# A hybrid mixer layer on one core: the sums of the second half's x^T are formed in the first half and kept in DRAM

## The chip, the cores and the metric

The kernel runs on one NeuronCore of one Trainium2 chip. The metric is the device time of one execution in microseconds (us), as the median of several runs. TensorE (PE) multiplies matrices, VectorE (DVE), ScalarE (ACT) and GpSimd (POOL) work on tiles, and SyncE (SP) issues nearly all DMA transfers, one queue in program order.

## The reference, cut to what matters

```
xn = rms_norm(x, ln_g)                        # x: (2048, 1024)
proj = xn @ w_in                              # w_in: (1024, 6144), six groups of 1024 columns
b_gate, c_gate, x_conv, g_conv, x_lru, g_lru = split(proj)
y_conv = norm(b_gate * conv3(c_gate * x_conv)) * silu(g_conv)
y_lru  = norm(rg_lru(x_lru)) * silu(g_lru)    # a scan over the 2048 positions
h = x + concat(y_conv, y_lru) @ w_out         # w_out: (2048, 1024)
return rms_norm(h, final_g)
```

## The kernel before, in words

The large products are done in float32 by a scheme of Strassen's kind: a product of 2x2 blocks needs seven products of sums of blocks instead of eight. One operand is the *set* T, the other the weights S. A set holds, for j = 0 to 3, seven *parts* (i, j), each 128x512, made from the four blocks b11, b12, b21, b22 of a pair of row blocks (row blocks j and j+4 of x^T, two halves of 512 positions):

- parts 0, 4 and 5 are b11, b21 and b22 themselves;
- part 3 is b22-b12, part 2 is b12-b11, part 1 is b22 minus part 2, part 6 is b21 minus part 1.

Each part is *split* into two float32r tiles: ACT casts it to `th` (a CAST, "hi"), DVE subtracts to get the rest `tl` (a TENSOR_TENSOR at L160, "lo"). Three matmuls (s.th, s.tl, s.th) per part and j make the product; all are at L877, 128x512 each.

The work is a list of 64 steps: 24 for the first half of the positions (for k = 0 to 7 a step "l" for the linear recurrent unit, "a" and "b" for the short convolution), 24 for the second half, 16 of the output projection. Each half, and each half of the output projection, has its own set T; where one follows the other the set *changes*. A step has seven or eight slots, each starting with `tick()`, which runs the functions that `at(slots, f)` put down some slots earlier. All engines run in the order in which this code issues their instructions. In a steady step the slots multiply parts 0, 6 (of the step before), 1, 3, 2, 4, 5 in turn. ACT copies the intermediate products out of PSUM to q1, u2 and rr. These are single buffers: the copy to u2 of the next step must wait until DVE has read the old u2 (in `put(21, ...)`, the operation `gb<-bank,u` for a step "b"), and PE must wait for that copy before it goes on adding to the same bank.

**x^T of the second half.** In the first half, `second_half` reads the rows of the second half of x (`rows`), gets their norms (`root`, stored to DRAM as `rsx`), and then in 16 calls of `cols(c, kt)`, four in every 21 slots (one k), loads a broadcast of the norms and one block of x^T, scales it on DVE (L515) and stores it to `xnd`. So `xnd` holds the 16 scaled blocks.

**The change to the second half's set.** During the two steps ahead of it and in its first step, `load_t` loads the four blocks of a j from `xnd`, and `TPrep` forms the sums on DVE and splits the parts. j = 0 is spread over the slots of the last step of the first half; j = 1 to 3 are done by `whole()` inside the first step of the new half. That first step (`if jm:`) goes through j from 0 to 3 in the outer loop, with six PSUM banks open, so that PE can start with the parts of j = 0.

**The changes to the two sets of the output projection** use `TParts` instead: there the sums of the weight blocks lie ready in DRAM, each part is loaded into one of eight `raw` buffers (name `traw`), and `parts(n)` splits the parts up to the n-th, two at a time (two casts, two subtractions), and loads up to six parts ahead. Their order puts twelve parts, of j = 0 and 1, ahead of the first step.

The tag `hl` has four 128x1024 buffers, which `st`, `qh`, `ql` of the steady steps share with `xcol`; `aux` has four 128x512 buffers. The last slots of a step "b" and the first of the next "l" carry, on DVE and behind each other: the gates and the scan of the recurrent unit, the splits of the next weights, and the reads of PSUM.

Of the kernel before, what the change touches and what calls it, by code (L numbers as in the profile page):

```python
# [12 lines left out]
F32 = mybir.dt.float32  # L13
# [25 lines left out]
def hymba_kernel(ctx: ExitStack, tc: tile.TileContext, x, xt, w_in, par, lamc, w_gate, w_out, final_g, out):  # L39
# [16 lines left out]
    xnd = [dram.tile([KT, P, C], F32, name=f"xnd{c}") for c in range(2)]  # L56
# [173 lines left out]
    class TPrep:  # L230
# [3 lines left out]
        def add(self, i):  # L234
            b11, b12, b21, b22 = (self.r.get(n) for n in range(4))
            t = self.t
            if i == 2:
                t[2] = aux("t1")
                tt(t[2], b12, b11, ALU.subtract)
            elif i == 1:  # L240
                t[1] = aux("t2")
                tt(t[1], b22, t[2], ALU.subtract)
            elif i == 3:
                tt(b12, b22, b12, ALU.subtract)
            else:
                tt(t[1], b21, t[1], ALU.subtract)


        def whole(self):
            b11, b12, b21, b22 = (self.r[n] for n in range(4))  # L250
            self.t = {1: b22, 2: b11, 6: b21}
            for i in (0, 5, 4):
                self.hi(i)
            self.lo(0)
            tt(b11, b12, b11, ALU.subtract)
            self.lo(5)
            tt(b12, b22, b12, ALU.subtract)
            self.hi(2)
            self.hi(3)
            tt(b22, b22, b11, ALU.subtract)  # L260
            self.hi(1)
            self.lo(4)
            self.lo(1)
            tt(b21, b21, b22, ALU.subtract)
            self.hi(6, b21)
            self.lo(3)
            self.lo(2)
            self.lo(6, None, b21)

# [189 lines left out]


    def load_t(j, r, only=range(4)):
        for n in only:
            i, q = ((0, 0), (0, 1), (1, 1), (1, 0))[n]
            kt = j + i * NB
            r[2 * i + q] = piece("traw")
            nc.sync.dma_start(r[2 * i + q], xnd[q][kt])
# [28 lines left out]
    def second_half():  # L495
# [13 lines left out]
        def cols(c, kt):  # L509
            t2 = wt("hl", "xcol", bufs=HL)  # L510
            rb, t = t2[:, 0:C], t2[:, C:2 * C]
            nc.sync.dma_start(rb.rearrange("p (b q) -> p b q", b=NB),
                              rsx[c].rearrange("(o b) p -> o b p", o=1).broadcast_to((P, NB, P)))
            nc.sync.dma_start(t, xt[kt * P:(kt + 1) * P, (2 + c) * C:(3 + c) * C])
            at(3, lambda: nc.vector.scalar_tensor_tensor(  # L515
                out=t, in0=t, scalar=pt[:, LN_G + kt:LN_G + kt + 1], in1=rb,
                op0=ALU.mult, op1=ALU.mult))
            at(5, lambda: nc.sync.dma_start(xnd[c][kt], t))
# [392 lines left out]
    with tc.manual_schedule(engines={ENG.PE, ENG.Activation, ENG.DVE, ENG.Pool, ENG.SP}):  # L911
# [173 lines left out]
        for n in range(PLAIN, N):  # L1085
# [9 lines left out]
            if jm:  # L1095
                bk = {}
                for j in range(NB):
# [6 lines left out]
                    if Tq is not None and j < 3:  # L1104
                        Tq.parts((14, 21, 28)[j])
                    elif j == 0:
                        Tp[0].hi(6)
                        Tp[0].lo(6)
                        load_t(2, Tp[2].r)
                    elif j == 1:  # L1110
                        load_t(3, Tp[3].r)
                    if Tq is None and j < 3:
                        Tp[j + 1].whole()
# [25 lines left out]
            for s in range(8 if new or last else 7):  # L1139
# [15 lines left out]
                if nx == 1:  # L1155
                    if soon and s == 4:
                        Tp = [TPrep(q, {}, T2) for q in range(NB)]
                        load_t(0, Tp[0].r)
                    if new:
                        if s == 1:  # L1160
                            Tp[0].hi(0)
                            Tp[0].lo(0)
                        elif s == 2:
                            for q in (2, 1, 3):
                                Tp[0].add(q)
                        elif s == 3:
                            load_t(1, Tp[1].r)
                            Tp[0].hi(1)
                        elif s == 4:
                            Tp[0].hi(3)  # L1170
                            Tp[0].lo(1)
                        elif s == 5:
                            Tp[0].hi(2)
                            Tp[0].lo(3)
                            Tp[0].add(6)
# [96 lines left out]
```

## Time and profile before

| | before |
|---|---|
| median of 3 runs | 1426.95 us (1425.71 to 1427.22) |
| the profiled execution | 1426.31 us, span 1424.5 us |
| PE busy | 1335.4 us, 94% of the span |
| DVE busy | 1069.8 us, 75% |
| ACT, POOL busy | 782.0 us (55%), 258.4 us (18%) |
| DMA | 371.02 MB, mean 260 GB/s |
| mean granted TensorE clock | 0.982 |

Busy shares are means over stages with different limits; a stage is read from the windows and from the instructions in order of time. "Idle before, released by" in square brackets names what an engine waited for. In the window lines the columns are the window, its length, the busy time and count of PE, weight loads, DVE, ACT and POOL, then the granted TensorE clock (1.00 is full), the busy share of the DMA engines and GB/s.

### The profile page before, as it was taken

To read this page: it belongs to the slowest core of one execution; us is meant where nothing else is said; L and a number is where in the kernel's file an instruction comes from. 1 tells how busy PE (TensorE), PEld (TensorE's weight loads), DVE (VectorE), ACT (ScalarE), POOL (GpSimd) and SP (SyncE) were. 2 spreads that over 40 slices of the span, in tenths; PEclk is the share of its full clock that TensorE was granted. 3 is DMA by queue.
4 is the path that set the end of the run, shared out by engine and by line. 5 is a ranking of instruction groups with operands and counts; after the bars stand their busy time and mean duration, and the time that the engine had idled before them with its cause. 6 is when DMAs were issued, how large, how long until landed. Compare 5 with 4: busy or idle time off the path is not lost.

```text
span 1424.5 us, 16977 instructions
## 1 busy us (share of the span) xinstructions
PE 1335.4 (94%) x5732; PEld 1068.4 (75%) x5732; DVE 1069.8 (75%) x1264; ACT 782.0 (55%) x1165; POOL 258.4 (18%) x168
## 2 busy tenths in 40 slices
PE   5979999999999997899998999899996999989997
PEld 4867777778787775677886878687874788868885
DVE  5788887998989889777767667665657548668885
ACT  6576668566665756475563645463646323434442
POOL 2414343434534331001000000101010000000000
PEclk9999999999999998999999999999998999989999
DMA  5137797987978866631899999998978999698643
GB/s 212 30 110 259 271 275 239 284 322 273 328 275 297 305 246 220 225 102 38 276 313 339 332 342 326 347 315 307 288 269 330 348 292 278 215 403 292 216 156 122
DMA packets 165190, 371.02 MB, mean 260 GB/s; under 512 B 17264, under 2 KB 52464, under 8 KB 165104
## 3 DMA queue, kind: packets, MB, share of 16 engines
q1 hardware_dynamic: 164672, 369.63, 75.7%
q8 instruction: 45, 0.74, 0.2%
q14 instruction: 41, 0.34, 0.1%
q10 hardware_dynamic: 432, 0.32, 0.1%
HBM read 224.45 MB, written 145.43 MB: 260 GB/s over the span
## 4 chain that ended last, share of the span: by engine, by line
PE 63%; DVE 11%; DMA 10%; ACT 10%; issue 3%; SPq 2%; POOL 0%; DVEq 0%; ACTq 0%
PE bank L877 59%; DVE s L160 2%; ACT i L668 2%; PE gate L661 2%; DMA traw<-in_w_out_dram 2%; ACT r L668 2%; PE norm_ps L554 2%; DVE tl L160 2%; DMA sd<-s 1%; DVE traw L160 1%; DVE r L695 1%; DMA zr<-rsd 1%; DMA so<-so 1%; DMA s<-sd 1%; ACT q L1208 1%
## 5 line engine op out<-in xcount | busy, mean ns | idle before, releaser
L877 PE MATMUL bank<-th,s 128*128 128x512 f32 x3608 | 1145.6, 394 | 43.1 <-DMA s<-so 8.8
L877 PEld LDWEIGHTS bank<-th,s 128*128 128x128 f32 x3608 | 683.4, 189 | 207.5 <-issue 14.5
L877 PE MATMUL bank<-tl,s 128*128 128x512 f32 x1804 | 709.7, 393 | 7.1 <-DVE tl L160 6.5
L877 PEld LDWEIGHTS bank<-tl,s 128*128 128x128 f32 x1804 | 341.7, 189 | 83.2 <-DVE tl L160 11.7
L160 POOL TENSOR_TENSOR s<-raw,s 128x512 fp32r<-128x512 f32 x67 | 127.2, 1911 | 263.2 <-ACT s L197 217.1
L197 ACT CAST s<-raw 128x512 fp32r<-128x512 f32 x136 | 81.9, 617 | 56.9 <-PE bank L877 39.8
L1211 ACT COPY u<-bank 128x512 f32<-128x512 f32 x58 | 34.0, 587 | 140.1 <-PE bank L877 90.2
L160 POOL TENSOR_TENSOR gb<-gb,sg 128x1024 f32<-128x1024 f32 x16 | 42.5, 2658 | 352.4 <-ACT sg L594 296.1
L160 DVE TENSOR_TENSOR s<-s,s 128x512 fp32r<-128x512 f32 x102 | 100.6, 986 | 5.4 <-ACT s L197 5.4
L160 DVE TENSOR_TENSOR tl<-traw,th 128x512 fp32r<-128x512 f32 x98 | 66.5, 705 | 46.9 <-ACT th L454 29.4
L160 DVE TENSOR_TENSOR s<-raw,s 128x512 fp32r<-128x512 f32 (+1 forms) x115 | 86.6, 777 | 9.9 <-ACT s L197 5.3
L1208 ACT COPY q<-bank 128x512 f32<-128x512 f32 x58 | 33.8, 583 | 83.0 <-PE bank L877 75.8
L160 DVE TENSOR_TENSOR raw<-raw,zr 128x512 f32<-128x512 f32 x64 | 47.9, 769 | 36.8 <-DMA zr<-rsd 36.8
L197 ACT CAST s<-s 128x512 fp32r<-128x512 f32 x102 | 62.8, 616 | 7.5 <-DVE s L160 7.4
L635 DVE SCALAR_TENSOR_TENSOR u<-xl,pt,u 128x1024 f32<-128x1024 f32 x48 | 65.4, 1363 | 0.7 <-ACT u L631 0.2
L1214 ACT COPY rr<-bank 128x512 f32<-128x512 f32 x58 | 33.9, 584 | 45.7 <-PE bank L877 45.6
L745 DVE SCALAR_TENSOR_TENSOR t<-p,pt,t 128x1024 f32<-128x1024 f32 x32 | 48.5, 1517 | 4.9 <-ACT t L742 4.1
L160 DVE TENSOR_TENSOR st<-u,st 64x1024 fp32r<-64x1024 f32 x32 | 50.9, 1590 | 1.0
L160 POOL TENSOR_TENSOR gl<-gl,sg 128x1024 f32<-128x1024 f32 x16 | 45.6, 2849 | 14.4 <-ACT sg L594 14.4
L631 ACT ACTIVATE u<-xl,pt 128x1024 f32<-128x1024 f32 x16 | 19.9, 1246 | 48.1 <-DVE xl L160 48.0
L160 DVE TENSOR_TENSOR ob<-bank,rr 128x512 f32<-128x512 f32 x18 | 12.2, 689 | 44.7 <-ACT rr L1214 44.7
L668 ACT ACTIVATE r<-gate,pt 64x512 f32<-64x512 f32 x64 | 43.7, 683 | 1.7 <-PE gate L661 1.1
(161 smaller groups left out, 1372.2 us busy)
## 6 DMA issues: line engine op xcount, KB each, us to landing
sd<-s SPq DMA_DIRECT2D x147, 512.0 KB, 4.8
s<-sd SPq DMA_DIRECT2D x147, 512.0 KB, 6.0
raw<-in_w_in_dram SPq DMA_DIRECT2D x108, 256.0 KB, 4.7
so<-so SPq DMA_DIRECT2D x42, 512.0 KB, 6.2
s<-so SPq DMA_DIRECT2D x42, 512.0 KB, 7.5
raw<-yd SPq DMA_DIRECT2D x64, 256.0 KB, 5.8
traw<-in_w_out_dram SPq DMA_DIRECT2D x56, 256.0 KB, 5.9
yd<-gl SPq DMA_DIRECT2D x32, 256.0 KB, 3.7
```

What stands on the lines that cost most here:

```text
L160: (eng or nc.vector).tensor_tensor(out=out, in0=a, in1=b, op=op)
L197: nc.scalar.copy(dst[i][0], val(i))
L554: nc.tensor.matmul(norm_ps[0], sel[:, s0:s0 + R], q[:, i * C:(i + 1) * C], start=norm_ps[1] == 0, stop=norm_ps[1] == 8 * KT - 1)
L631: nc.scalar.activation(out=v["u"], in_=o1[:, 1:1 + N2], func=AF.Identity, scale=lw[0], bias=pt[:, LB + k:LB + k + 1])
L635: nc.vector.scalar_tensor_tensor(out=v["u"], in0=o1[:, 1 + j:1 + j + N2], scalar=lw[j], in1=v["u"], op0=ALU.mult, op1=ALU.add)
L661: nc.tensor.matmul(ps[j], v["gw"][n][:, j, :], v["st"][j][:, sl], start=(n == 0), stop=(n == 1))
L668: nc.scalar.activation(out=g_[hi, sl], in_=v["ps"][j][src], func=AF.Sigmoid, bias=pt[src, bias + k:bias + k + 1])
L745: nc.vector.scalar_tensor_tensor(out=tcur["t"], in0=p[:, 2 + j:2 + j + N2], scalar=cw[j], in1=tcur["t"], op0=ALU.mult, op1=ALU.add)
L877: nc.tensor.matmul(bank, a[:, js], b, start=start and n == 0, stop=stop and n == 2, skip_group_check=more)
L1208: nc.scalar.copy(q1, bk["A"])
L1211: nc.scalar.copy(u2, bk["A"])
L1214: nc.scalar.copy(rr, bk["A"])
```

## The change

`cols` is replaced by `block(j)`, called four times, once in the step "b" of each k from 3 to 6 (slot 3). It loads both halves of x^T's row blocks j and j+4 and of the norms' broadcast into three `xcol` buffers (six DMAs of 256 KB), scales two 128x1024 tiles on DVE two slots later (`scale`), forms the four sums with four 128x512 subtractions one slot after that (`add`), and stores the seven parts in four DMAs two slots later (`store`). `xnd[j]` now holds seven parts. The change to the second half's set uses `TParts`, which loads each part ready to split; with n = 1 its order puts the seven parts of j = 0 first, then j = 1, 2, 3. `TPrep.add`, `TPrep.whole` and `load_t` are gone.

```diff
-    xnd = [dram.tile([KT, P, C], F32, name=f"xnd{c}") for c in range(2)]
+    xnd = [dram.tile([7, P, C], F32, name=f"xnd{j}") for j in range(NB)]
...
     class TParts:
-            self.order = [(i, j) for i in ORDER for j in range(2)]
-            self.order += [(i, j) for j in (2, 3) for i in ORDER]
+            n = 1 if t == 1 else 2
+            self.order = [(i, j) for i in ORDER for j in range(n)]
+            self.order += [(i, j) for j in range(n, NB) for i in ORDER]
...
-                w = w_blocks(self.t, j)
-                src = {0: w[0], 4: w[2], 5: w[3]}.get(i)
+                w = w_blocks(self.t, j) if self.t > 1 else None
+                src = {0: w[0], 4: w[2], 5: w[3]}.get(i) if w else xnd[j][(0, 3, 4, 5, 2, 1, 6).index(i)]
...
-        def cols(c, kt):
-            ...
+        def block(j):
+            a, b, r = [wt("hl", "xcol", bufs=HL) for _ in range(3)]
+            for c in range(2):
+                cs = slice(c * C, (c + 1) * C)
+                nc.sync.dma_start(r[:, cs].rearrange("p (b q) -> p b q", b=NB),
+                                  rsx[c].rearrange("(o b) p -> o b p", o=1).broadcast_to((P, NB, P)))
+                for t, kt in ((a, j), (b, j + NB)):
+                    nc.sync.dma_start(t[:, cs], xt[kt * P:(kt + 1) * P, (2 + c) * C:(3 + c) * C])
+            def scale():
+                for t, kt in ((a, j), (b, j + NB)):
+                    nc.vector.scalar_tensor_tensor(out=t, in0=t, scalar=pt[:, LN_G + kt:LN_G + kt + 1],
+                                                   in1=r, op0=ALU.mult, op1=ALU.mult)
+            def add():
+                ...
+                tt(t2, b12, b11, ALU.subtract)
+                tt(b12, b22, b12, ALU.subtract)
+                tt(t1, b22, t2, ALU.subtract)
+                x_.append(aux("t6"))
+                tt(x_[0], b21, t1, ALU.subtract)
+            def store():
+                for n, t in enumerate((a, b, r)):
+                    nc.sync.dma_start(xnd[j][2 * n:2 * n + 2].rearrange("h p c -> p h c"),
+                                      t.rearrange("p (h c) -> p h c", h=2))
+                nc.sync.dma_start(xnd[j][6], x_[0])
+            at(2, scale)
+            at(3, add)
+            at(5, store)
...
-        for c in range(2):
-            for kt in range(KT):
-                at(free.pop(1) - 7, lambda c=c, kt=kt: cols(c, kt))
+        for j in range(NB):
+            at(21 * (3 + j) + 17 - 4, lambda j=j: block(j))
...
-                    if Tq is not None and j < 3:
+                    if j < 3:
                         Tq.parts((14, 21, 28)[j])
-                    ...
-                    if Tq is None and j < 3:
-                        Tp[j + 1].whole()
...
-                if nx == 1:
-                    ...
+                if nx:
                     if soon and s == 5:
                         Tq = TParts(nx, T2)
                         Tq.load(4)
                     if new and s in (1, 3, 4, 5, 6, 7):
-                        Tq.parts(2 * (1, 3, 4, 5, 6, 7).index(s) + 2)
+                        Tq.parts(((1, 3, 4, 5, 6, 7).index(s) + 1) * (1 if nx == 1 else 2))
```

PE's instructions and POOL's stand in the same order as before. The first place is DVE from the middle of a step "b" into the next "l". `xcol` is x^T being scaled, `t<-bank,t`, `u` and `r` belong to the two mixers, `s` are weights being split. Before, one scaling stands on either side of the scan; three rows behind the last one follows the read `gb<-bank,u`:

```order
L515 SCALAR_TENSOR_TENSOR xcol<-xcol,pt 128x512
L160 TENSOR_TENSOR s<-raw,s 128x512
L160 TENSOR_TENSOR s_2965<-raw,s_2965 128x512
L160 TENSOR_TENSOR q_2956<-bank,q_2956 128x512
L160 TENSOR_TENSOR t<-q_2956,t 128x512
L686 SCALAR_TENSOR_TENSOR u<-r,u 128x1024
L160 TENSOR_TENSOR s<-s_2963,s 128x512
L160 TENSOR_TENSOR t<-bank,t 128x512
L160 TENSOR_TENSOR u<-T,u 128x1024
L695 SCALAR_TENSOR_TENSOR r<-r,u 128x1024
L698 COPY hl<-r 128x1
L515 SCALAR_TENSOR_TENSOR xcol<-xcol,pt 128x512
```

Now both wide scalings and all four sums (the last goes to `t`, which is t6) stand ahead of the scan, and so ahead of `gb<-bank,u`, which again comes three rows behind the `hl` copy:

```order
L478 SCALAR_TENSOR_TENSOR xcol<-xcol,pt 128x1024 x2
L160 TENSOR_TENSOR s<-raw,s 128x512
L160 TENSOR_TENSOR s_2964<-raw,s_2964 128x512
L160 TENSOR_TENSOR q_2955<-bank,q_2955 128x512
L160 TENSOR_TENSOR t<-q_2955,t 128x512
L667 SCALAR_TENSOR_TENSOR u<-r,u 128x1024
L160 TENSOR_TENSOR xcol<-xcol 128x512 x3
L160 TENSOR_TENSOR t_3102<-xcol 128x512
L160 TENSOR_TENSOR s<-s_2962,s 128x512
L160 TENSOR_TENSOR t<-bank,t 128x512
L160 TENSOR_TENSOR u<-T,u 128x1024
L676 SCALAR_TENSOR_TENSOR r<-r,u 128x1024
```

Two further scalings, one earlier in the same "b" and one a few operations behind `gb<-bank,u`, are gone too. The second place is SP's queue at the same point: `sd` are stores of split weights, `raw` loads of weights. Before, the loads and stores of the blocks are strewn between them:

```order
L512 DMA xcol<-rsx_93 128x512
L514 DMA xcol<-in_xt_dram 128x512
L202 DMA sd_113<-s 128x1024
L331 DMA raw<-in_w_in_dram 128x512 x4
L202 DMA sd_113<-s 128x1024
L512 DMA xcol<-rsx_93 128x512
L514 DMA xcol<-in_xt_dram 128x512
L518 DMA xnd_95<-xcol 128x512
```

Now six loads stand together in front of four loads of weights, and four stores together behind:

```order
L471 DMA xcol<-rsx_92 128x512
L474 DMA xcol<-in_xt_dram 128x512 x2
L471 DMA xcol<-rsx_93 128x512
L474 DMA xcol<-in_xt_dram 128x512 x2
L295 DMA raw<-in_w_in_dram 128x512 x4
L202 DMA sd_115<-s 128x1024 x2
L202 DMA sd_116<-s 128x1024 x3
L494 DMA xnd_96<-xcol 128x2x512 x3
L496 DMA xnd_96<-t_3634 128x512
```

The loads moved past one another into one group, and the stores behind the sums. The third place is DVE in the first step of the second half. Before, sums (`traw<-traw`) stand between the subtractions of the split (`tl`):

```order
L565 SCALAR_TENSOR_TENSOR gl<-r,pt,gl 128x1024
L160 TENSOR_TENSOR tl<-t_4592,th 128x512
L160 TENSOR_TENSOR tl<-traw,th 128x512
L160 TENSOR_TENSOR traw<-traw 128x512
L160 TENSOR_TENSOR tl<-traw,th 128x512
L160 TENSOR_TENSOR traw<-traw 128x512 x2
L160 TENSOR_TENSOR tl<-traw,th 128x512 x2
L160 TENSOR_TENSOR traw<-traw 128x512
L160 TENSOR_TENSOR tl<-traw,th 128x512 x4
```

Now the subtractions follow each other, 22 in all:

```order
L546 SCALAR_TENSOR_TENSOR gl<-r,pt,gl 128x1024
L160 TENSOR_TENSOR tl<-traw,th 128x512 x15
L160 TENSOR_TENSOR ql<-r,qh 128x1024
L546 SCALAR_TENSOR_TENSOR gb<-t,pt,gb 128x1024
L160 TENSOR_TENSOR tl<-traw,th 128x512 x7
```

The twelve sums of this step are gone, and the parts come in the order in which PE uses them.

More of the change, by code (lines that the diff above doesn't have):

```diff
@@ L232, in __init__ @@
             self.j, self.r, self.dst, self.t = j, r, dst, {}
[L234 to L268, printed above, removed]
         def val(self, i):
@@ L458, in parts @@
                 self.load(min(28, self.split + 6))
[L461 to L466, printed above, removed]
     def rstd(rs, ss):
@@ L507, in root @@
             at(3, lambda: nc.sync.dma_start(rsx[c].rearrange("b p -> p b"), rs[c]))
-        def cols(c, kt):
[L510 to L518, printed above, removed]
+        def block(j):
[10 more added lines that the diff above has]
+                                                   in1=r, op0=ALU.mult, op1=ALU.mult)
+            x_ = []
+            def add():
+                b11, b12, b21, b22 = a[:, 0:C], a[:, C:2 * C], b[:, 0:C], b[:, C:2 * C]
+                t2, t1 = r[:, 0:C], r[:, C:2 * C]
+                tt(t2, b12, b11, ALU.subtract)
[11 more added lines that the diff above has]
+            at(5, store)
         free = [21 * k + s + 2 for k in range(KT) for s in (2, 15, 17, 20) if 21 * k + s > 20]
@@ L1103, in hymba_kernel @@
                         prep(n, 7)
-                    if Tq is not None and j < 3:
+                    if j < 3:
                         Tq.parts((14, 21, 28)[j])
[L1106 to L1111, printed above, removed]
-                    if Tq is None and j < 3:
-                        Tp[j + 1].whole()
                     if j == 2:
@@ L1154, in hymba_kernel @@
                     T2 = {}
-                if nx == 1:
[L1156 to L1175, printed above, removed]
-                        elif s == 6:
-                            Tp[0].hi(4)
-                            Tp[0].lo(4)
-                            Tp[0].lo(2)
-                        elif s == 7:
-                            Tp[0].hi(5)
-                            Tp[0].lo(5)
-                elif nx:
+                if nx:
                     if soon and s == 5:
```

## The prediction

> **What bounds the kernel now.** I read the page's busy times first, then windows by stage: one k of the first half (its three steps), and the first step of the second half, where the set changes.
>
> ```profile
> PE 1335.4 (94%) x5732; PEld 1068.4 (75%) x5732; DVE 1069.8 (75%) x1264; ACT 782.0 (55%) x1165; POOL 258.4 (18%) x168
> ```
> ```profile
> 304.80:367.40 62.60, 61.86 (x269) 49.65 (x269) 57.33 (x58) 40.48 (x59) 25.63 (x15) 1.00 0.83 296
> 346.00:349.00 3.00, 3.00 (x15) 2.49 (x14) 2.24 (x2) 2.92 (x6) 2.99 (x2) 1.00 0.31 87
> 551.10:583.50 32.40, 18.95 (x55) 12.22 (x56) 29.80 (x42) 17.15 (x28) 3.17 (x1) 0.79 0.31 100
> ```
>
> In the first half PE is the bound: it is busy 61.86 of 62.60 us, 0.233 us for each of 269 matmuls. DVE is close behind with 57.33 us (92%). At the change, the 55 matmuls of j = 1 to 3 (three for each of six parts, and one) would take 55 x 0.233 = 12.8 us at that pace and take 32.4: about 19.6 us are lost there, with DVE busy 29.80. So the change moves DVE work from a stage that waits for DVE into one in which PE waits for nothing and DVE has 62.60 - 57.33 = 5.3 us in 62.6 to spare. The question is where in those 62.6 us the added work stands.
>
> **The change, part by part. First the block's sums on DVE.** The instructions in order of time, DVE from the middle of a step "b" to the read `gb<-bank,u`, with one later `u<-T,u` for comparison; then POOL, ACT and PE at the same place:
>
> ```profile
> 351.38 0.69 DVE L160 TENSOR_TENSOR gb<-bank,rr 128x512 f32<-128x512 f32 x1 [0.71 <-ACT rr L1214]
> 351.99 0.74 DVE L515 SCALAR_TENSOR_TENSOR xcol<-xcol,pt 128x512 f32<-128x512 f32 x1
> 352.65 1.29 DVE L160 TENSOR_TENSOR s<-raw,s 128x512 fp32r<-128x512 f32 x2
> ...
> 357.52 2.15 DVE L160 TENSOR_TENSOR u<-T,u 128x1024 f32<-128x1024 f32 x1
> ...
> 362.12 1.50 DVE L515 SCALAR_TENSOR_TENSOR xcol<-xcol,pt 128x512 f32<-128x512 f32 x1
> 363.55 1.77 DVE L160 TENSOR_TENSOR s<-raw 128x512 f32<-128x512 f32 x1
> 365.36 0.69 DVE L160 TENSOR_TENSOR s<-s,raw 128x512 f32<-128x512 f32 x1
> 365.96 0.68 DVE L160 TENSOR_TENSOR gb<-bank,u 128x512 f32<-128x512 f32 x1
> ...
> 547.62 1.22 DVE L160 TENSOR_TENSOR u<-T,u 128x1024 f32<-128x1024 f32 x1
> ```
> ```profile
> 360.03 4.74 POOL L160 TENSOR_TENSOR s<-raw,s 128x512 fp32r<-128x512 f32 x2 [1.40 <-ACT s L197]
> ```
> ```profile
> 366.74 0.58 ACT L1211 COPY u<-bank 128x512 f32<-128x512 f32 x1 [4.55 <-DVE gb L160]
> ```
> ```profile
> 367.38 0.50 PE L877 MATMUL bank<-th,s 128*128 128x512 f32 x1 [0.41 <-ACT u L1211]
> ```
>
> From 351.38 to 365.96 DVE has no idle time. ACT waits 4.55 us for the end of `gb<-bank,u`, because u2 is one buffer, and PE already waits 0.41 us for ACT's copy. What is added to DVE between 351.38 and 365.96 reaches PE one for one. The order shows that all of the block's DVE work stands there. Prices, from start to start, right behind that place:
>
> ```profile
> 366.56 1.28 DVE L565 SCALAR_TENSOR_TENSOR gl<-r,pt,gl 128x1024 f32<-128x1024 f32 x1
> 367.76 0.68 DVE L160 TENSOR_TENSOR s<-s,s 128x512 fp32r<-128x512 f32 x1
> 368.36 0.69 DVE L160 TENSOR_TENSOR raw<-raw 128x512 f32<-128x512 f32 x1
> 368.96 0.75 DVE L515 SCALAR_TENSOR_TENSOR xcol<-xcol,pt 128x512 f32<-128x512 f32 x1
> ```
>
> A wide scaling costs 367.76 - 366.56 = 1.20 us, a sum 0.60. Added: 2 x 1.20 + 4 x 0.60 = 4.80 us. Removed from the same stretch: the scalings at 351.99 (0.66 to the next start) and 362.12 (1.43). The second takes 1.50 us instead of 0.75 because POOL works on SBUF from 360.03 to 364.77; the next operation takes 1.77 instead of about 0.69. POOL's work stays, so its 0.77 us fall on whatever DVE does then: I count 0.66 for it too. Net 4.80 - 1.32 = 3.48, say 3.5 us for each block. Lower bound 4.80 - 0.66 - 1.43 = 2.7; upper bound 3.5 + 1.1 = 4.6, if one more sum is stretched like the 1.77 us operation. The scalings that went elsewhere in this k (0.75 us at 368.96) give nothing: DVE waits for ACT there soon after, as it does at 351.38.
>
> PE's gap becomes 0.41 + 3.5 = 3.9 us, once per k, four times. A gap also costs clock. PE's rows behind gaps of 6.40 and 3.30 us, and the windows that begin there and behind one of 2.06 us (its row, 568.78, stands below):
>
> ```profile
> 83.00 0.76 PE L661 MATMUL gate<-st,bh 128*128 128x512 f32 x1 [6.40 <-ACT hp L750]
> 1275.42 0.76 PE L877 MATMUL bank<-th,s 128*128 128x512 f32 x1 [3.30 <-DMA s<-so]
> ```
> ```profile
> 83.00:86.85 3.85, 3.79 (x9) 2.57 (x9) 3.78 (x3) 3.50 (x6) 1.27 (x1) 0.52 0.19 79
> 568.78:573.16 4.38, 3.91 (x14) 2.65 (x15) 4.38 (x7) 2.19 (x4) 0.00 (x0) 1.00 0.00 0
> 1275.42:1281.47 6.05, 6.05 (x15) 4.76 (x16) 4.14 (x6) 0.51 (x2) 0.00 (x0) 0.51 1.03 395
> ```
>
> After 6.40 and 3.30 us PE ran at 0.52 and 0.51 of its clock and lost 3.85 - 9 x 0.233 = 1.75 and 6.05 - 15 x 0.233 = 2.55 us; after 2.06 us it stayed at 1.00. A gap of 3.9 us lies on the slow side: I take 2.0 us, near the middle of the two losses, with 0 and 2.55 as ends. Four blocks: 4 x (3.5 + 2.0) = 22 us lost (ends 4 x 2.7 = 11 and 4 x 7.15 = 29).
>
> The Trainium skill ("TensorE: Matmul & The Clock Gate", Part 1) says that the clock is halved after at least one idle window of about 3.4 us, and that the windows run freely. By that, few gaps of 3.9 us would hold a whole window, and the 2.0 would mostly be 0; the row at 1275.42 went slow after 3.30 us, so I go by the row and keep the other as a rival.
>
> **The block's transfers.** The last gate matmuls, which read `st`, SP's row, and the landing times of `xcol`'s transfers and then of `xnd`'s:
>
> ```profile
> 341.73 0.50 PE L661 MATMUL gate<-st,bh 128*128 128x512 f32 x1 [0.16 <-ACT i L668]
> ```
> ```profile
> 339.08 8.04 SPq L331 DMA_DIRECT2D raw<-in_w_in_dram  x4
> ```
> ```profile
> DMA to landing us min/median/max: 2.0/5.4/7.7
> ```
> ```profile
> DMA to landing us min/median/max: 2.0/4.3/6.9
> ```
>
> Six loads (1.5 MB) go ahead of the four `raw` loads, which hold SP for 8.04 us for a buffer while the DMA is 0.31 busy (346 to 349). The last `xcol` buffer comes free with the gate matmuls at 341.73, some 9 us ahead of the scaling at about 352, against a landing of 5.4, at most 7.7: no cost, and 2 us per block as the other end, should the last of the six land that late. Then DVE holds everything behind the scaling. The four stores wait for the sums; behind them wait stores of weights, the `yd` stores and `raw` loads, which the code first reads five slots later. In bytes a block loads 1.5 MB instead of 2 and stores 1.75 instead of 1: +0.25 MB in 62.6 us at 296 GB/s, hidden at a DMA share of 0.83.
>
> **The change of the set.** PE's gaps there and DVE beside them; then the same first step at the next change, which uses `TParts` already:
>
> ```profile
> 556.72 0.79 PE L877 MATMUL bank<-tl,s 128*128 128x512 f32 x1 [4.01 <-DVE tl L160]
> 560.10 0.79 PE L877 MATMUL bank<-th,s 128*128 128x512 f32 x1 [2.16 <-ACT th L277]
> 568.78 0.49 PE L877 MATMUL bank<-th,s 128*128 128x512 f32 x1 [2.06 <-ACT th L277]
> 578.15 0.74 PE L877 MATMUL bank<-th,s 128*128 128x512 f32 x1 [2.57 <-ACT th L277]
> ```
> ```profile
> 552.35 3.12 DVE L565 SCALAR_TENSOR_TENSOR gl<-r,pt,gl 128x1024 f32<-128x1024 f32 x1
> 555.39 0.68 DVE L160 TENSOR_TENSOR tl<-t,th 128x512 fp32r<-128x512 f32 x1
> ...
> 571.77 1.22 DVE L160 TENSOR_TENSOR ql<-r,qh 128x1024 fp32r<-128x1024 f32 x1
> 572.91 1.28 DVE L565 SCALAR_TENSOR_TENSOR gb<-t,pt,gb 128x1024 f32<-128x1024 f32 x1
> 574.11 0.68 DVE L160 TENSOR_TENSOR tl<-traw,th 128x512 fp32r<-128x512 f32 x1
> ...
> 1093.88 3.11 DVE L565 SCALAR_TENSOR_TENSOR gl<-r,pt,gl 128x1024 f32<-128x1024 f32 x1
> ...
> 1112.00 0.69 DVE L160 TENSOR_TENSOR tl<-traw,th 128x512 fp32r<-128x512 f32 x1 [0.51 <-ACT th L454]
> ```
>
> The first gap (4.01) is the scan's and `gl`'s, ahead of the split in both kernels; it stays. Behind 555.39 there follow 22 splits of 0.60 us and `ql` and `gb` (574.11 - 571.77 = 2.34): 15.5 us, so the last split ends near 571 and PE with it, instead of 583.5: a gain of 12.5 us. At the next change, from `gl`'s start to the last split's end, it took 1112.69 - 1093.88 = 18.8 us with 16 splits; with six more (3.6) that puts our end at 552.35 + 22.4 = 574.8, a gain of 8.7. PE may then wait for the next weights, which SP now issues behind 16 loads of parts: 3.30 us at the third change (1275.42). 28 loads instead of 16 are +3 MB in a stretch at 100 GB/s, landing in 4.3 us with eight buffers: room enough. Gain 10 us, between 5.4 (8.7 - 3.3) and 12.5.
>
> **Sum.** +22 - 10 = +12 us on the profiled execution's 1426.31 us, which is 0.64 below the median: 1438.3 there, 1439 as a median. What a measurement of this kernel tells from no change is about 0.2%, 2.9 us.
>
> **Rivals.**
> - *Clock stays.* The 3.9 us gaps do not slow PE: 4 x 3.5 - 10 = +4, 1431 us. For it: 1.00 after 2.06 us. Against: 0.51 after 3.30. It is what the Trainium skill's rule above would give.
> - *Faster: the port is free.* POOL's share falls away from DVE's stretch: 0.93 us of `u<-T,u` (2.15 against 1.22), 0.77 and 1.09 of the two after 362.12, 2.8 in all. Then a block adds 3.5 - 2.8 = 0.7 us, PE's gap is 1.1 and the clock holds: 4 x 0.7 - 10 = -7, 1420 us. It decides from less than 2.5 us lost per block. For it: the sums and the scan change places against POOL's operations. Against: ACT's casts, not DVE, start POOL, so it works in the same stretch.
> - *Late transfers.* The block's loads land 2 us late, or the parts come at the slower pace: +8, 1447 us. Against: the 0.31 above.
>
> **How the numbers follow.** Forecast 0.50 (1434 to 1446), clock stays 0.17 (1427 to 1434), late 0.12 (1446 to 1455), faster 0.18 (1416 to 1424), all terms small 0.03. From 1418 to 1449 the range takes in the forecast, the clock rival, half of the late and most of the faster one; the likeliest one's own is 1434 to 1446. Slower by over 0.2%: 0.50 + 0.12 + 0.13 = 0.75; same 0.06; faster 0.19.
>
> **What would show it.** A PE wait for ACT's u2 copy of about 3.9 us, once in each of the four k that have a block, followed by a clock near 0.5; the `gb<-bank,u` ahead of it 3.5 us later than now, measured from `gb<-bank,rr`. In the new half's first step DVE's splits one after the other and PE's end near 572 from a start as now. I am wrong if those four gaps stay under 2 us, or if the first step still takes over 28 us from 551.10's place.

## The result, and the profile after

The changed kernel takes 1442.26 us (median of four runs, 1440.78 to 1447.30) against 1426.97 for the kernel before beside it: a ratio of 1.0112 (95% interval 1.0094 to 1.0129), 15.3 us slower. The forecast was 1439, with 1418 to 1449 as the range. The profiled execution took 1442.50 us, with a span of 1440.7.

The page's busy times hardly move: DVE and PE do nearly the same work in a longer time.

```profile
PE 1336.6 (93%) x5732; PEld 1072.7 (74%) x5732; DVE 1072.1 (74%) x1256; ACT 784.0 (54%) x1165; POOL 250.8 (17%) x168
```

The windows by stage say where: one k that holds a block, and then the first step of the second half, from the start of its first gap to its end.

```profile
377.05:445.02 67.97, 63.15 (x268) 50.85 (x268) 59.81 (x60) 40.74 (x59) 23.29 (x15) 0.97 0.77 277
572.55:598.15 25.60, 16.64 (x55) 12.34 (x55) 22.06 (x30) 17.55 (x28) 3.19 (x1) 0.80 0.61 207
```

A k behind a block's gap takes 67.84 to 67.97 us instead of 62.60. When the first step of the new set begins, 572.55 - 551.10 = 21.45 us have been lost; that step then takes 25.60 us instead of 32.40. A mark that all of the traces share is the first gate matmul of the second half that has to wait (the release by ACT's `i` is in its row), behind both places (before, then after):

```profile
611.70 0.50 PE L661 MATMUL gate<-st,bh 128*128 128x512 f32 x1 [0.69 <-ACT i L668]
```
```profile
626.37 0.50 PE L642 MATMUL gate<-st,bh 128*128 128x512 f32 x1 [0.70 <-ACT i L649]
```

So 14.7 of the 16.2 us between the two spans have been lost by then. In the table below this mark stands beside the time, since it takes in both places and little else. It comes from one execution, the time from several.

**In the block's k.** PE's timeline has the forecast gap in all four k, two of which are these, and DVE's timeline has its cause, the block's work between `gb<-bank,rr` and `gb<-bank,u`; ACT's copy to u2 waits for the latter.

```profile
309.21 0.79 PE L858 MATMUL bank<-th,s 128*128 128x512 f32 x1 [4.66 <-ACT u L1156]
377.05 0.60 PE L858 MATMUL bank<-th,s 128*128 128x512 f32 x1 [4.66 <-ACT u L1156]
```
```profile
356.82 0.69 DVE L160 TENSOR_TENSOR gb<-bank,rr 128x512 f32<-128x512 f32 x1 [0.96 <-ACT rr L1159]
...
363.48 4.21 DVE L160 TENSOR_TENSOR xcol<-xcol 128x512 f32<-128x512 f32 x3
367.72 1.80 DVE L160 TENSOR_TENSOR t<-xcol 128x512 f32<-128x512 f32 x1
...
370.65 1.21 DVE L160 TENSOR_TENSOR u<-T,u 128x1024 f32<-128x1024 f32 x1
...
374.30 0.69 DVE L160 TENSOR_TENSOR s<-raw 128x512 f32<-128x512 f32 x1
...
375.64 0.68 DVE L160 TENSOR_TENSOR gb<-bank,u 128x512 f32<-128x512 f32 x1
```
```profile
376.41 0.59 ACT L1156 COPY u<-bank 128x512 f32<-128x512 f32 x1 [8.80 <-DVE gb L160]
```

From the one read to the other it is 375.64 - 356.82 = 18.82 us, against 365.96 - 351.38 = 14.58 before: 4.24 us more, and PE's gap is 4.66 - 0.41 = 4.25 us longer. The four sums take 5.97 us (from 363.48 to the next start, 369.45), not 2.4. The groups of the tile (count, then minimum/median/maximum of one in ns) and POOL's timeline beside them:

```profile
L160 DVE TENSOR_TENSOR xcol<-xcol x12: 692/1780/1784, 295.6 to 501.8; 128x512 f32<-128x512 f32 x12
```
```profile
362.72 1.99 POOL L160 TENSOR_TENSOR s<-raw,s 128x512 fp32r<-128x512 f32 x1 [8.78 <-ACT s L197]
...
365.46 1.69 POOL L160 TENSOR_TENSOR s<-raw,s 128x512 fp32r<-128x512 f32 x1 [0.70 <-ACT s L197]
367.69 1.28 POOL L160 TENSOR_TENSOR s<-raw,s 128x512 fp32r<-128x512 f32 x1 [0.55 <-ACT s L197]
```

Of the four sums in each block, one takes 0.69 us alone and three take 1.78 to 1.80, each beside one of POOL's three operations. In exchange `u<-T,u` takes 1.21 us (2.15 before) and `s<-raw` 0.69 (1.77 before): POOL's share of DVE's time has gone from those to the sums. The loads cost nothing here: DVE has no wait for a DMA from 250 to 550 us.

Behind the gap PE runs at a lower clock: 20 and 19 matmuls in 6 us instead of 6.00 / 0.233 = 25.8. In the first 4 us behind each of the four gaps the granted clock is 0.50 to 0.60.

```profile
309.21:315.21 6.00, 6.00 (x20) 4.85 (x21) 4.25 (x5) 5.96 (x8) 2.40 (x1) 0.73 0.85 306
377.05:383.05 6.00, 6.00 (x19) 4.77 (x20) 4.25 (x5) 5.96 (x8) 2.40 (x1) 0.72 0.84 294
```

**At the change of the set.** PE's two long gaps, DVE's start of `gl` and its last splits, who waited for the parts' loads, what those loads (L411) waited for on SP's queue (us, times; then the longest), and two windows:

```profile
578.17 0.79 PE L858 MATMUL bank<-tl,s 128*128 128x512 f32 x1 [4.03 <-DVE tl L160]
592.76 0.80 PE L858 MATMUL bank<-tl,s 128*128 128x512 f32 x1 [2.57 <-DVE tl L160]
```
```profile
573.78 3.14 DVE L546 SCALAR_TENSOR_TENSOR gl<-r,pt,gl 128x1024 f32<-128x1024 f32 x1
...
592.01 4.30 DVE L160 TENSOR_TENSOR tl<-traw,th 128x512 fp32r<-128x512 f32 x7
```
```profile
  ACT th L419: 5.6, 7
```
```profile
SPq L411 <- DVE tl L160: 10.3, 10, 6.2
```
```profile
575.00:580.00 5.00, 1.82 (x4) 1.49 (x5) 5.00 (x7) 3.82 (x6) 0.83 (x1) 0.53 0.22 73
592.76:595.50 2.74, 2.74 (x7) 2.16 (x8) 2.74 (x5) 2.29 (x4) 0.00 (x0) 0.50 0.20 30
```

From the start of `gl` to the end of the last split it is 596.31 - 573.78 = 22.5 us; the forecast had 18.7 and 22.4 as its two bases. ACT's casts waited seven times for a part's DMA. From 560 to 600 us SP in turn waited ten times, 10.3 us in all, for a split to free one of the eight buffers, and from 575 to 580 us the DMA was only 0.22 busy. PE's last matmul of the step ends 598.15 - 596.31 = 1.84 us behind the last split; behind its last gap PE runs at a granted clock of 0.50.

### The profile page after: what moved, and what is told of

Its sections match the earlier page's. It is cut to its first block, busy times and chain, and to the rows that moved or that the text cites. A ratio compares the mean times of both kernels' runs of the same rounds, so it can differ in the third digit from the quotient of the medians.

```text
span 1440.7 us, 16975 instructions
## 1 busy us (share of the span) xinstructions
PE 1336.6 (93%) x5732; PEld 1072.7 (74%) x5732; DVE 1072.1 (74%) x1256; ACT 784.0 (54%) x1165; POOL 250.8 (17%) x168
## 4 chain that ended last, share of the span: by engine, by line
PE 55%; DMA 16%; DVE 14%; ACT 8%; issue 4%; SPq 2%; POOL 1%; DVEq 0%; ACTq 0%; POOLq 0%
PE bank L858 51%; DMA s<-so 3%; DVE s L160 2%; DMA raw<-yd 2%; DMA yd<-gl 2%; DMA zr<-rsd 2%; PE gate L642 2%; PE norm_ps L535 2%; ACT i L649 2%; DMA sd<-s 2%; ACT r L649 2%; DVE r L676 1%; DVE xcol L160 1%; DVE traw L160 1%; DMA traw<-in_w_out_dram 1%
## 5 line engine op out<-in xcount | busy, mean ns | idle before, releaser
L160 POOL TENSOR_TENSOR s<-raw,s 128x512 fp32r<-128x512 f32 x67 | 118.6, 1780 | 271.9 <-ACT s L197 198.2
L1156 ACT COPY u<-bank 128x512 f32<-128x512 f32 x58 | 34.0, 587 | 159.6 <-PE bank L858 88.3
L160 DVE TENSOR_TENSOR s<-raw,s 128x512 fp32r<-128x512 f32 (+1 forms) x115 | 90.0, 807 | 10.0 <-ACT s L197 5.3
L419 ACT CAST th<-traw 128x512 fp32r<-128x512 f32 x84 | 49.5, 619 | 27.3 <-DMA traw<-td 9.5
L1159 ACT COPY rr<-bank 128x512 f32<-128x512 f32 x58 | 33.9, 585 | 44.9 <-PE bank L858 44.8
L160 DVE TENSOR_TENSOR xx<-bank,u 128x512 f32<-128x512 f32 x15 | 10.4, 691 | 46.9 <-PE bank L858 46.9
```

The source lines that it names most:

```text
L160: (eng or nc.vector).tensor_tensor(out=out, in0=a, in1=b, op=op)
L419: nc.scalar.copy(self.dst[i, j][0], self.r[i, j])
L1156: nc.scalar.copy(u2, bk["A"])
L1159: nc.scalar.copy(rr, bk["A"])
```

## The experiments

The first theory (A): the loss is DVE work ahead of `gb<-bank,u`, passed on to PE through the single u2 buffer. Its rivals: DVE is too full in these k, so that the wait turns up elsewhere whatever is moved (B); the block's transfers cost (C). The kernel before took 1426.5 to 1427.2 us (medians) beside these runs.

### How much work, and whose

Without the block's DVE work (transfers and set change stay):

```
-                tt(t2, ...); tt(b12, ...); tt(t1, ...); x_.append(aux("t6")); tt(x_[0], ...)
+                x_.append(b21)
...
-            at(2, scale)
```

> The changed kernel without the block's two scalings and four sums on DVE (left out; the columns are stored as they were loaded, seven tiles of the same size from the same places), with all of its loads and stores and the new set change. Theory A (DVE work): the four gaps are gone, what is left is the set change's gain of about 7 us and 0.41 us per k: 1417 to 1421 us. Rival C (the transfers take part in the loss): the time stays above 1426, with waits for a DMA or for raw buffers in those k.

Without the sums (the scalings stay), and with six sums:

```
-                tt(t2, ...); tt(b12, ...); tt(t1, ...); x_.append(aux("t6")); tt(x_[0], ...)
+                x_.append(b21)
```

> The changed kernel without the block's four sums (left out: the scaled columns are stored in their place, seven tiles of the same size); the two wide scalings, all transfers and the new set change stay. If the sums are the larger part of the loss: DVE's stretch ahead of gb<-bank,u loses the sums' 5.97 us and gets back some 2.9 us, by which POOL then stretches s<-s, u<-T,u and the scan (as in the run with the sums later); the gap behind the u2 copy falls from 4.66 to about 1.6, without a second one behind rr: 4 x (3.1 + about 1) less than 1442, so 1424 to 1428 us. If the scalings alone make the loss: over 1434. If DVE's first 1.1 us net are free: near the 1413.6 of the run without any of the block's DVE work.

```
                 tt(x_[0], b21, t1, ALU.subtract)
+                tt(x_[0], b21, t1, ALU.subtract)
+                tt(x_[0], b21, t1, ALU.subtract)
```

> The changed kernel with the last sum of each block computed three times: six sums in the place of four, same result, same transfers. If DVE's work at this place reaches PE one for one at the price of an undisturbed sum (0.60 us, since POOL has finished its splits when they run): the four gaps grow from 4.66 to about 5.9, 4 x 1.2 = 4.8 us and up to 1 us of clock each: 1446 to 1451 us. If each sum at this place costs the 1.4 to 1.8 us that the four took there: gaps of 7.5 to 8.3, 1454 to 1460 us. If some of the work is hidden: under 1444.

One pair of DVE instructions exchanged, in step l: the read first, then the weight sums:

```
-                if s > 0:
+                if s > 0 and not (s == 1 and kind == "l"):
                     prep(n + 1, s - 1)
...
                         put0(21, B, u20)
                         pend = None
+                    if kind == "l":
+                        prep(n + 1, 0)
```

> The changed kernel with one pair of DVE instructions moved: in step l, gb<-bank,u is put ahead of the two weight sums s<-raw and s<-s,raw (0.73 and 0.61 us from start to start) that stand ahead of it now. If DVE's work ahead of gb<-bank,u reaches PE one for one, the four gaps fall by 1.34 us, from 4.66 to 3.3, and the time by 4 x 1.34 to 4 x 1.9: 1434 to 1437 us. If the wait then shows up at the rr copy, because the weight sums that are now behind feed ACT's casts ahead of it (as with the sums later): a second gap of 1 to 1.4 us there and 1439 to 1443.

Measured (gap: PE's idle time ahead of the matmul behind the u2 copy; mark: the gate matmul named above):

| kernel | us | ratio to before (95%) | gap, us | mark, us |
|---|---|---|---|---|
| no block work on DVE | 1413.64 | 0.9906 (0.9885 to 0.9926) | none over 0.2 | 598.63 |
| scalings, no sums | 1424.89 | 0.9978 (0.9962 to 0.9993) | 1.59 | 609.30 |
| changed, read first | 1432.39 | 1.0040 (1.0024 to 1.0057) | 3.32 | 617.53 |
| changed | 1442.26 | 1.0112 (1.0094 to 1.0129) | 4.66 | 626.37 |
| six sums | 1448.62 | 1.0143 (1.0110 to 1.0176) | 6.12 | 633.10 |

The window of one k without the block's DVE work, and the gaps without the sums, with the read first and with six sums in PE's timelines:

```profile
340.62:402.10 61.48, 61.31 (x269) 49.73 (x269) 54.63 (x54) 40.50 (x58) 25.63 (x15) 1.00 0.84 306
```
```profile
370.33 0.50 PE L854 MATMUL bank<-th,s 128*128 128x512 f32 x1 [1.59 <-ACT u L1152]
```
```profile
373.63 0.50 PE L858 MATMUL bank<-th,s 128*128 128x512 f32 x1 [3.32 <-ACT u L1158]
```
```profile
381.10 0.80 PE L860 MATMUL bank<-th,s 128*128 128x512 f32 x1 [6.12 <-ACT u L1158]
```

DVE's work ahead of the read reaches PE one for one. Two weight sums of 1.34 us put behind it take 1.34 us off the gap, as expected (the time is 1.6 us under what was expected; in the profiled execution the clock held behind one of the four gaps, as the last section shows, which is worth about 1.2 us). Without the four sums the gap is 3.07 us shorter: their 5.97 us less the 2.9 us that POOL then takes from their neighbours (the rows are as in the next run). Two more sums, which run when POOL is done, add 1.46, or 0.73 each (0.60 expected), to DVE's stretch and to the gap alike. The wide scalings, less the two small ones that they replace, make the rest, 1.59 - 0.41 = 1.18. Rival C falls: with all of its transfers, and no DVE work, a k takes 61.48 us, less than the 62.60 before, at a DMA share of 0.84 against 0.83; its stores, however, do not wait for sums. That run came 3 us under what was expected. In part this is because the short gaps of the kernel before had cost more than their length (last section); the rest is open. With the scalings but no sums, the change as a whole gains 2.3 us; the sums turn that into a loss.

### Can the wait be taken away instead?

The four sums three slots later:

```
-            at(3, add)
-            at(5, store)
+            at(6, add)
+            at(8, store)
```

> The changed kernel with each block's four sums (and, two slots behind them, their stores) moved three slots on: on DVE they now stand behind gb<-bank,u and gl, ahead of a split s<-s,s, with the same loads, scalings, bytes and set change. Theory A (the loss is DVE work that stands ahead of gb<-bank,u, passed on through the single u2 buffer): the sums take 5.97 us of that stretch, some 2 us of it come back because POOL then stretches u<-T,u and s<-raw again as before, so the four PE gaps of 4.66 us fall to about 0.7 to 1.5, and the time from 1442 to 1422 to 1427 us. Rival B (DVE is simply too full in these k, so that the wait turns up at the split behind the sums): PE waits 2 to 4 us for DVE's s instead, 1434 to 1442. Rival C (the block's transfers cost, not its sums): the gaps stay, 1440 to 1444.

1436.48 us, ratio 1.0060 (1.0039 to 1.0080), mark 620.96. The gap behind u2 is 1.59 us, near what A says (0.7 to 1.5), but the time is 9 us and more over A's. DVE's timeline ahead of `gb<-bank,u` and behind it, POOL beside it, then ACT and PE:

```profile
361.88 1.78 DVE L160 TENSOR_TENSOR s<-s,s 128x512 fp32r<-128x512 f32 x1
...
364.19 2.05 DVE L160 TENSOR_TENSOR u<-T,u 128x1024 f32<-128x1024 f32 x1
366.27 3.27 DVE L676 TENSOR_TENSOR_SCAN r<-r,u 128x1024 f32<-128x1024 f32 x1
...
374.83 2.93 DVE L160 TENSOR_TENSOR t<-xcol 128x512 f32<-128x512 f32 x1
```
```profile
374.80 2.41 POOL L160 TENSOR_TENSOR gb<-gb,sg 128x1024 f32<-128x1024 f32 x1 [7.41 <-DVE xcol L160]
```
```profile
379.04 0.62 ACT L197 CAST s<-raw 128x512 fp32r<-128x512 f32 x1 [1.77 <-DVE raw L160]
```
```profile
380.20 0.64 PE L858 MATMUL bank<-th,s 128*128 128x512 f32 x1 [2.07 <-ACT rr L1159]
```

POOL's three splits now stretch `s<-s` (1.78 against 0.68 in the changed kernel), `u<-T,u` (2.05 against 1.21) and the scan (3.27 against 2.29): 2.92 us. And the sums delay `raw<-raw`, for whose cast ACT waits 1.77 us; the rr copy stands behind that cast in ACT's queue, and PE waits 2.07 us for it. (`t<-xcol` takes 2.93 us beside POOL's operation and holds `raw<-raw`.) With the two gaps and the clock a k takes 67.24 us. That is rival B's second gap.

The other side of the wait, u2 and rr in turn, so that ACT's u2 copy takes the buffer that was read long ago:

```
-                    u2 = sm("u2")
+                    u2 = sm(("u2", "rr")[n % 2])
...
-                    rr = sm("rr")
+                    rr = sm(("rr", "u2")[n % 2])
```

> The changed kernel, in which u2 and rr change their two buffers from step to step, so that ACT's copy to u2 no longer waits for the gb<-bank,u of the step before but for that step's rr, which is read several us earlier. DVE's order and work stay. Theory A: the four PE gaps behind ACT's u2 copy vanish (under 0.5 us) although the sums stand where they stood, and 4 x (4.66 + about 1 of slow clock) goes: 1419 to 1424 us. Rival B (DVE is too full): the sums delay what DVE does next, and PE waits 2 to 4 us for that, 1432 to 1440. Rival C (transfers): 1438 to 1444.

1436.84 us, ratio 1.0069 (1.0051 to 1.0086). The mark stands at 626.79: in the first half the exchange wins nothing, and the 5 us came later in the program, where the block has no part. ACT's and PE's timelines:

```profile
368.58 0.59 ACT L1156 COPY rr<-bank 128x512 f32<-128x512 f32 x1 [2.15 <-PE bank L858]
...
375.17 1.06 ACT L575 ACTIVATE sg<-gb 128x1024 f32<-128x1024 f32 x1 [4.70 <-DVE gb L160]
...
380.30 0.58 ACT L1159 COPY u<-bank 128x512 f32<-128x512 f32 x1
```
```profile
380.93 0.79 PE L858 MATMUL bank<-th,s 128*128 128x512 f32 x1 [4.29 <-ACT u L1159]
```

The copy of the line for u2 (L1156) no longer waits for DVE. But the next thing in ACT's queue is the sigmoid `sg<-gb`, which reads what `gb<-bank,u` wrote; ACT waits 4.70 us for the same DVE instruction there, and the copy that PE needs next (L1159) comes 5.1 us behind it, 1.00 us of which is a further wait of ACT for DVE (`raw<-raw`). The gap is 0.37 us shorter than in the changed kernel, but the clock behind it is 0.50 for 4 us, and a k takes 68.4 to 68.6 us. Theory A's path was one of two. The same exchange in the kernel before:

> The kernel before with the same exchange of the buffers of u2 and rr. Theory A: only the waits of 0.41 us per k go, and others of that kind at most: 1422 to 1427 us, so that the exchange is worth under 5 us here and some 20 in the changed kernel. If the exchange is worth 15 to 20 us here too, the cause is not the block.

1418.44 us, ratio 0.9930 (0.9911 to 0.9950), mark 607.05: 8 us faster, more than A had expected. No gap over 0.2 us is left in k = 3 to 7, and a k takes 61.8 us. So the exchange takes away a short delay, and of a long one only the part up to ACT's next wait for DVE.

A new theory (A2): each piece of DVE work costs by what ACT has queued behind it, so the sums cost nothing if neither `gb<-bank,u` nor `raw<-raw` stands behind them. Both edits together, with the sums four slots later (`at(7, add)`, `at(8, store)`):

> The changed kernel with both edits: u2 and rr change buffers from step to step, and the four sums stand four slots later, behind gl, s<-s,s and raw<-raw, so that neither gb<-bank,u nor the raw<-raw on whose cast ACT waits ahead of the rr copy stands behind them; the stores follow one slot behind. Theory A2 (PE loses only through what ACT has queued ahead of its copies, so each DVE piece costs by its place): no gap over 0.7 us in the four k, 1414 to 1421 us, under the kernel before. Rival B (DVE has no room for 4.8 us more in a k, wherever they stand): gaps of 2 us or more at another place, 1426 to 1436. A wait of ql for the buffers that the block's stores still hold would be B's first sign.

1443.11 us, ratio 1.0104 (1.0075 to 1.0132), mark 631.93: A2 fell as well, and B's range (1426 to 1436) was too low. SP's queue, DVE and PE:

```profile
380.12 1.80 SPq L494 DMA_DIRECT2D xnd<-xcol  x3
382.02 1.19 SPq L496 DMA_DIRECT2D xnd<-t  x1
383.25 2.15 SPq L551 DMA_DIRECT2D yd<-gl  x2
```
```profile
388.43 0.69 DVE L160 TENSOR_TENSOR gl<-bank,u 128x512 f32<-128x512 f32 x1 [5.32 <-DMA yd<-gl]
```
```profile
390.31 0.44 PE L535 MATMUL norm_ps<-ql,sel 128*64 128x512 f32 x1 [4.34 <-DVE ql L160]
```

The block's four stores wait for the sums, and `yd<-gl` is queued behind them on SP; DVE waits 5.32 us until it has landed, since the next `gl` uses its buffer, and PE 4.34 us for `ql` behind that. So the transfers do cost, where the stores come late.

The last try on this line put the exchange and the early read together in the changed kernel:

> The changed kernel with u2 and rr in turn and gb<-bank,u ahead of the two weight sums. In the run with u2 and rr in turn PE waited 4.29 us for the rr copy, which ACT has queued behind sg<-gb, a square and two casts (5.1 us), and sg waited 4.70 us for gb<-bank,u. If ACT's order behind gb<-bank,u makes that wait, 1.34 us less reach PE: gaps of about 2.9, 1428 to 1433 us. If another DVE result in ACT's queue (gl, raw<-raw) holds the chain, the gap stays at 4 or more: 1434 to 1438.

1436.15 us, ratio 1.0066 (1.0042 to 1.0089), mark 625.38: the second of the two cases expected. The gap was not 2.9 us but 5.03, longer than with the exchange alone (4.29). DVE's, ACT's and PE's rows:

```profile
374.20 3.41 DVE L546 SCALAR_TENSOR_TENSOR gl<-r,pt,gl 128x1024 f32<-128x1024 f32 x1
```
```profile
377.64 1.06 ACT L555 ACTIVATE r<-r 128x1024 f32<-128x1024 f32 x1 [2.70 <-DVE gl L546]
```
```profile
380.83 0.80 PE L858 MATMUL bank<-th,s 128*128 128x512 f32 x1 [5.03 <-ACT u L1161]
```

The earlier sigmoid starts POOL's `gb<-gb,sg` earlier (374.13 us), now beside `gl`, which takes 3.41 us instead of 1.28; the square that ACT has ahead of the copy waits for `gl`.

In each of these four versions of the changed kernel PE waits at another place for DVE's lateness, as rival B says. Rival B in its strict form, that no order has room, is not shown: DVE is busy 59.8 of 68 us.

### The set change

Without the loads of the parts of j = 1 to 3 (the splits read tiles of j = 0 in their place):

```
+                if self.t == 1 and j > 0:       # load(): no piece, no DMA
+                    self.r[i, j] = None
+                    continue
...
+                    if self.r[i, j] is None:    # parts(): split th of j = 0
+                        self.r[i, j] = self.dst[i, 0][0].bitcast(F32)
```

> The changed kernel, which at the change to the second half's set leaves out the loads of the 21 parts with j = 1 to 3 (it splits the th tiles of j = 0 in their place, so the second half's x is wrong from there; instructions of ACT and DVE and their number stay). If the waits of ACT's casts for the parts' DMA (5.6 us in seven waits) are what kept the set change from gaining more: the stretch from the first gap to the last matmul falls from 25.6 to 20 to 22.5 us and the time to 1437 to 1440. If DVE's chain (gl, 22 splits, ql and gb) sets it anyway: 25 to 26 us, and the time stays within 1441 to 1444.

1437.30 us, ratio 1.0065 (1.0046 to 1.0085), mark 622.72. The window of the first step, DVE's `gl` and its last splits:

```profile
574.22:594.51 20.29, 14.76 (x55) 11.46 (x55) 20.26 (x28) 16.10 (x27) 3.18 (x1) 0.83 0.19 61
```
```profile
575.39 3.13 DVE L551 SCALAR_TENSOR_TENSOR gl<-r,pt,gl 128x1024 f32<-128x1024 f32 x1
...
589.81 4.29 DVE L160 TENSOR_TENSOR tl<-th 128x512 fp32r<-128x512 f32 x7
```

Without the loads the step takes 20.3 us instead of 25.6, and DVE is busy in all of it. From `gl` to the last split it is 594.10 - 575.39 = 18.7 us instead of 22.5, and PE ends 0.4 us behind the last split instead of 1.84. The missing part of the gain is the parts' loads. Whether more buffers or an earlier start of the loads would bring it was not tried.

### A faster version

The early read alone, and both edits, in the kernel before:

> The kernel before with the same edit. Its gaps of 0.41 us and the small one behind rr go in the k with scalings, and of those of about 1.0 us at k = 1 and 2 the part that DVE makes: like the exchange of u2 and rr (1418.4 us), 1418 to 1423 us. If it comes to 1426 or more, the wait only moves to the rr copy also here.

> The kernel before with both edits (u2 and rr in turn, gb<-bank,u ahead of the weight sums): a try at a faster version without the change. With u2 and rr in turn alone no gap over 0.2 us is left in k = 3 to 7, so the second edit should add little: 1416 to 1420 us. If the weight sums that are now later make ACT's casts late, 1420 to 1424.

The early read alone takes 1421.03 us, ratio 0.9960 (0.9947 to 0.9974), both edits 1416.13 us, ratio 0.9927 (0.9904 to 0.9950); the marks are 605.97 and 604.14. Both came out as expected. In the second a k is at the pace of the run without the block's DVE work:

```profile
342.00:403.50 61.50, 61.34 (x269) 49.58 (x268) 55.60 (x58) 40.74 (x59) 25.78 (x16) 1.00 0.85 300
```

At 1416.13 us it beats both kernels, with the old change of the set; the exchange of buffers alone (0.9930) is not told apart from it. No version with the sums in the first half came near it.

## Why the prediction was right, and where it was off

*The place and the path.* Right: PE waits for ACT's u2 copy in the four k, 4.66 us where 3.9 was forecast, with `gb<-bank,u` 4.24 us later where 3.5 was. That "what is added there reaches PE one for one" is shown by the runs with the read first, without the sums and with six. That it does so "because u2 is one buffer" was half of it: with u2 and rr in turn the wait is still 4.29 us, by ACT's order.

*The price of the sums.* The term of 3.5 us measured 4.24, inside its bounds of 2.7 to 4.6. The step that failed is the price of four sums at 0.60, with POOL's 0.77 put once on "whatever DVE does then". POOL has three operations there. The sums took 5.97 us, 3.57 more than counted; `u<-T,u`, `s<-raw` and the removed scaling gave back 0.94 + 1.08 + 0.77 = 2.79; the difference, 0.78, is what was missing. The rival "the port is free" counted this 2.8 as a gain and put nothing on the sums.

*The clock.* The forecast had the low clock right (0.50 to 0.60 in the first 4 us), but the 2.0 us for each gap were too much: PE is busy 63.02 to 63.15 us in a k against 61.86, so 1.2 to 1.3 us, 5 in all instead of 8. Reading a loss from rows behind two gaps elsewhere gave the right sign and the wrong size. The rival "clock stays" is wrong for these gaps, all four of which went slow.

*The transfers.* Right that they cost nothing where the change put them (61.48 us for a k with all of them, and no wait of DVE for a DMA in the block's k). They cost as soon as the stores come later; that was not asked of the forecast.

*The change of the set.* A gain of 10 us was forecast, 6.8 came (32.40 - 25.60). The step that failed is "landing in 4.3 us with eight buffers: room enough". The base of 18.7 us from `gl` to the last split is what the run without the loads shows; with them it took 22.5, since ACT waits 5.6 us for DMA and DVE then for ACT. That is the forecast's slower base of 22.4, which should have left a gain of 8.7. The other 1.9 us went because PE does not end "with it": its last matmul ended 1.84 us behind the last split. Twenty-two parts of 256 KB are 5.8 MB; at the 0.60 us of a split they would need 437 GB/s (an estimate), more than the 391 that the DMA moved at a busy share of 1.08 from 585 to 590 us. The forecast counted 3 MB more against a rate of 100 GB/s and did not ask at what rate the shorter step would need them. It did not ask either when the buffers come free: DVE frees none during the scan and `gl` (571.38 to 576.84 us), and from 575 to 580 us the DMA was 0.22 busy. Which of the two limits weighs more is open. The wait for the next weights, which the lower bound held, did not come.

*The sum.* 4 x 4.24 + 4 x 1.25 - 6.8 = +15.2 us; the mark moved by 14.7 and the medians differ by 15.3, against +12. Three terms were off, by +3.0, -3.0 and +3.2. The first two cancelled: the first half lost 21.45 us up to the change, with 22 forecast. That the total came within 3.3 us of the forecast is in part luck.

## What to carry to other kernels

When work is moved from a stage that waits for an engine into one where that engine is 92% busy, price it at its place: at the length it has beside the other engine's work there, and along every queue that stands behind it, the copy, the next activation and the stores. Taking away the wait that the profile names helps only if the next instruction in that queue does not wait for the same event; here the exchange of two buffers was worth 4.6 us by the mark in the kernel before, where the delay was 0.4 us, and nothing where it was 4.7. And for a stage made shorter, divide its bytes by the new time, not the old, and ask when the buffers for its loads come free.

## What the runs showed of the hardware

*DVE beside POOL.* One POOL operation of 1.28 us made one DVE sum 1.11 us longer (0.69 to 1.80), and one of 2.41 us made a sum 2.24 longer (2.93). The DVE instruction with two SBUF inputs that stood beside it paid, whichever it was, and the three operations took 2.8 to 3.6 us in all (2.8 in the kernel before, 2.92 with the sums later, 3.57 in the changed kernel). The Trainium skill ("SBUF — State Buffer", Who interferes with whom) says that a DVE instruction with two SBUF inputs contends with a GpSimd (POOL) instruction that reads SBUF, and that contention for the ports that the two share is an exclusive lock; the price of nearly one POOL operation each agrees with that.

*The clock behind a gap.* Gaps of the same length go either way. Windows of about 4 us behind gaps of 3.31 and 3.32 us (changed kernel, read first), then behind gaps of 2.03 and 2.07 us (sums later):

```profile
306.97:311.00 4.03, 4.03 (x11) 3.17 (x12) 4.03 (x5) 3.99 (x5) 1.63 (x1) 0.58 0.77 265
373.63:377.60 3.97, 3.97 (x17) 3.28 (x18) 3.97 (x5) 3.93 (x5) 1.57 (x1) 1.00 0.71 249
```
```profile
313.90:318.00 4.10, 4.09 (x18) 3.40 (x19) 1.72 (x2) 1.58 (x3) 1.29 (x1) 1.00 1.02 358
...
380.20:384.20 4.00, 4.00 (x11) 3.17 (x12) 1.73 (x2) 0.98 (x2) 1.28 (x1) 0.57 1.03 364
```

In the block's k of these traces, none of four gaps of 1.59 us went slow (no sums), two of four of 2.03 to 2.07 us (each with a gap of 1.59 us 7.8 us ahead of it), three of four of 3.31 and 3.32 us, and all twenty of 4.25 to 6.12 us (0.50 to 0.60 in the first 4 us). The Trainium skill ("TensorE: Matmul & The Clock Gate", Part 1) has a free-running window of some 3.4 us, which agrees with the chance in it. The gap of 2.07 us that was enough is shorter than the whole idle window that it asks for.

*A short gap costs more than its length.* Without gaps a k takes 61.48 us; before, with 0.41 and 0.18 us of gaps behind copies and a granted clock of 1.00, 62.60. About half of the 1.1 us is not idle time: PE is busy 61.86 us against 61.31, and the first matmul behind a gap takes 0.50 us (its end is modelled by the profile), against 0.233 from one to the next.
